# Moving weight subtractions off GpSimd and evictions ahead of weight roundings in a fused transformer layer

## The chip, the cores and the metric

The kernel runs on one core of one Trainium2 chip. A core has five engines that run side by side and meet only through semaphores: TensorE (matrix products into PSUM), VectorE (elementwise work with up to two tensors), ScalarE (activations and copies with a scale), GpSimd (elementwise work, and the queue from which adding transfers are issued) and SyncE, which issues plain transfers. The metric is the device time of one execution in microseconds. The kernel before takes 934.92 us, the median of three runs (934.16 to 937.03).

## The reference, cut to what matters

One layer of a diffusion backbone is applied to 128 context tokens and 512 latent tokens, which share all weights; the model width is 1024 and the MLP's is 4096.

```python
h = _rmsnorm(x, n1) * (1 + sc1) + sh1
aq, ak, av, bq, bk, bv, ga, gb = split(h @ w_in)          # 1024 -> 4352
a_o = _block_attention(aq, ak, av)                        # grouped-query attention
b_o = _neighbourhood_attention(bq, bk, bv, ...)           # 8 x 16 windows on the latent grid
m = sigmoid(ga) * (a_o @ w_br_a) + sigmoid(gb) * (b_o @ w_br_b)
x = x + g1 * (m @ w_out)                                  # the "out" products
h2 = _rmsnorm(x, n2) * (1 + sc2) + sh2
x = x + g2 * (square(relu(h2 @ w_mlp_in)) @ w_mlp_out)    # the MLP
y = _rmsnorm(x, final_norm_g)
```

Everything is float32. The shifts, scales and gates come from the conditioning vectors through another linear map.

## The kernel before

**Numbers in two parts.** TensorE works on a rounded form of float32. So that products keep their accuracy, each operand is held as a rounded high part and a low part, which is the rest: `hi = round(x)`, `lo = x - hi`. A product takes three matmuls: `wh*xh`, `wh*xl` and `wl*xh` (L321 to L323 and, in the MLP, L1646 to L1648). The high part is a copy on ScalarE that rounds. The low part can be made in three ways: by a subtraction on VectorE; by a subtraction on GpSimd; or by an adding transfer, for which ScalarE writes minus the rounded weight and a transfer issued by GpSimd adds the unrounded weight to it, from memory (L276) or from the staging tile (L1389).

**Tokens in two halves.** Activations lie transposed, 128 features in the partitions and 640 tokens in the free dimension, and are worked on in two halves of 320 tokens (h = 0 and 1). A matmul has 128 x 128 weights and 320 columns.

**Weights.** `W` feeds the weights of the projections, the branches and `out` in a fixed order (`w_order`). `conv` rounds one weight tile; `done` frees one and lets `ahead` round as many more as there are slots. `LOSET` (from `LOACC`) names the tiles whose low part comes by an adding transfer; `WPOOLSET` names those (`out` 4 to 7) that GpSimd subtracts.

**The out products.** The loop at L1608 takes 8 feature tiles n and both halves h: first (0,0), (0,1), (1,0) and so on to (3,1), then (4,0) to (7,0), then (4,1) to (7,1). `unit` runs the 24 matmuls of one and, in their middle and at their end, pops one entry each from the list `side`. Then `done` frees the weight (for h = 1) and thereby rounds further ones, `add_gated` (L1225) evicts the product from PSUM into the residual X1, and `sq_add` squares it on ScalarE and adds the square on VectorE to the sum `acc2` (L211), from which `rstd_half` gets the norm of that half. After (7,0) `side` holds that norm and four calls of `norm_first`, each of which scales two feature tiles of the first half (L1240), shifts them (L1246) and splits them in two parts (`cut`, L1273 and L1274). Up to here VectorE executes in the program's order (`manual_schedule`). The other engines, and VectorE from the MLP on, follow an order that a planner makes by its own estimates of when each instruction is ready.

**The MLP.** It is done in four chunks c of 1024 hidden features. In each, both layers are 2 x 2 block products that are computed with seven half-size products instead of eight (a Strassen form): A11, A12, S3, S2, A22, S1, S4, each for n = 0 to 3. A product is 12 matmuls. `FIRST0`, `FIRST1` and `FIRST2` write out their order by hand: (1,c,n,o) is one of layer 1, (2,c,n,o) one of layer 2. The right operands of S3, S2, A22 and S1 are sums of blocks; for layer 1 `t3_piece`, `t2_piece`, `t4_piece`, `t1_piece` and `n22_piece` make them from the normed halves, one feature tile k at a time, popped from `side`.

`Operands` brings the MLP's weights. Its loads come in strict order. An "A" load (SyncE, 512 KB, one of three staging tiles `wst`) holds the weights of A11 and A12. A "B" load (`wsb`, four tiles) holds a sum of weight blocks: GpSimd issues an adding transfer of 256 KB when it is loaded (L1371) and after the roundings of S3, S2 and A22 (L1394), which change it to the next product's weights. `conv` rounds one product's weights: the high part on ScalarE (L1386), the low part on VectorE or GpSimd (L1391) or by transfer (L1388, L1389). Rounding A12 or S4 frees the staging tile for the next load. Six rounded weight tiles `wb` are in flight at most. `evict` empties a product's bank, calls `ahead` for the next weights, runs what `later` has gathered and pops one entry from `side`.

Before the change GpSimd makes the low parts of A12 and A22 in layer 1 (`BLKPOOL`), 32 subtractions in all; VectorE makes the others, but for the last chunk's S4 of layer 2 (`LOTAIL`), which come by transfer.

Of the kernel before, what the change touches and what calls it, by code (L numbers as in the profile page):

```python
# [13 lines left out]
OP = mybir.AluOpType  # L14
# [5 lines left out]
KT = 8  # L20
# [32 lines left out]
NB = 4  # L53
NU = 6
NR = 5
BLKPOOL = (("A12", "A22"), ())
AUTO = (0, 0)
LAG3 = 5
POW = 0
SQP = 0  # L60
LOTAIL = tuple(("S4", n) for n in range(4))
NSUM = (1, 2)
TP = 4
TQ = 2
P3 = 8
GPV = 1
LOACC = (("in", 21, 22), ("in", 29, 30), ("in", 20, 23), ("in", 25, 26), ("in", 28, 34), ("br", 0, 8))
FINP = ()
HALVES = (slice(0, HT), slice(HT, NT))

# [2 lines left out]
def trunk_layer(ctx: ExitStack, tc: tile.TileContext, xT, small_in, wmodA, wmodB, tabs, cacheK, cacheV, bias,  # L73
                w_in, w_br, w_out, w1, w2, yT, akT, avT, bkT, bvT):
    nc = tc.nc
    PE, ACT, DVE = nc.tensor, nc.scalar, nc.vector
# [74 lines left out]
    def r32(ap):  # L151
        return ap.bitcast(F32)
# [53 lines left out]
    def sq_add(acc, x, f, sl):  # L206

        q = acc if f == 0 else u("sq")
        ACT.activation(q[:, sl], x[:, sl], AF.Square)
        if 0 < f < KT - 1:  # L210
            DVE.tensor_add(acc[:, sl], acc[:, sl], q[:, sl])  # L211
        return q

    def rstd_half(acc, last, rstd, sl):
# [19 lines left out]
    later = []  # L234
# [904 lines left out]
    class Units:  # L1139
        n = 0  # L1140
# [17 lines left out]
    for n in range(KT):  # L1158
# [4 lines left out]
        for i, w in enumerate((wa, wb)):  # L1163
            for h in range(2):
# [5 lines left out]
                ps = un.ps()  # L1170
# [51 lines left out]
    def add_gated(n, ps, h, chunk):  # L1222
        off = HALVES[h].start
        for sl, g in SEGS[h]:
            DVE.scalar_tensor_tensor(X1[n][:, sl], ps[:, sl.start - off:sl.stop - off], mod(chunk, n)[:, g:g + 1],  # L1225
                                     X1[n][:, sl], op0=OP.mult, op1=OP.add)

    T = [{}, {}, {}]
    L0, L1 = slice(0, HT), slice(HT, NT)
    RAW0, RAW1 = {}, []  # L1230

    def rstd2_half(last, h):
        return lambda: rstd_half(acc2, last, rstd2, HALVES[h])
# [37 lines left out]

    def cut(hi, lo, src):
        ACT.activation(hi, src, AF.Copy)  # L1273
        later.append(lambda: DVE.tensor_sub(lo, src, r32(hi)))  # L1274

    def cut_t(i, k, src):
        cut(T[i][k][:, L0], T[i][k][:, L1], src)
# [5 lines left out]

    def t2_piece(k):

        b11, b21, b12, b22 = RAW0[k][:, L0], RAW0[k][:, L1], RAW1[0][:, k], RAW1[0][:, k + 4]
        r = t_new(1, k)
        DVE.tensor_sub(b12, b12, b11)
        DVE.tensor_sub(r, b22, b12)
        DVE.tensor_sub(b21, b21, r)  # L1290
        cut_t(1, k, r)

    def t4_piece(k):
        cut(H2[k][0][:, L1], H2[k][1][:, L1], RAW0[k][:, L1])

    def t1_piece(k):
# [3 lines left out]
    def n22_piece(k):  # L1300
        f, b22 = k + 4, RAW1[0][:, k + 4]
        hi, lo = (t[:, L1] for t in H2[f])
        ACT.activation(hi, b22, AF.Copy, scale=-1.0)
        later.append(lambda: DVE.scalar_tensor_tensor(lo, b22, -1.0, r32(hi), op0=OP.mult, op1=OP.subtract))


    def natural(k0, sl):
# [32 lines left out]
    class Operands:  # L1340
# [38 lines left out]
        def conv(self):  # L1379
            self.feed()  # L1380
            l, c, n, o = SEQ[self.nc]
            k = (l, c, n, "A" if o in ("A11", "A12") else "B")
            t = self.st[k]
            t = t[:, 0:4] if o in ("A11", "S3", "S2", "S4") else t[:, 4:8]
            w = wp.tile([P, KT, P], F32R, tag="w" + "hl"[self.nc % 2], bufs=3, name="wb")
            ACT.activation(w[:, 0:4], t, AF.Copy)  # L1386
            if (l, c) == (2, 3) and (o, n) in LOTAIL:
                ACT.activation(w[:, 4:8], t, AF.Copy, scale=-1.0)  # L1388
                nc.gpsimd.dma_start(w[:, 4:8], t.bitcast(F32R), accum_op=OP.add)  # L1389
            else:  # L1390
                (nc.gpsimd if o in BLKPOOL[l - 1] else DVE).tensor_sub(w[:, 4:8], t, r32(w[:, 0:4]))  # L1391
            if o in ("S3", "S2", "A22"):
                e, half = {"S3": (1, 1), "S2": (0, 1), "A22": (1, 0)}[o]
                nc.gpsimd.dma_start(t, self.src(l, c, n, e)[:, 4 * half:4 * half + 4], accum_op=OP.add)  # L1394
            elif o in ("A12", "S4"):
                self.free(*k)
            self.t[SEQ[self.nc]] = w
            W.live += 1
            self.nc += 1
            self.feed()  # L1400
# [207 lines left out]
    for n, h in order(KT, 4):  # L1608
        if n not in Wt:
            Wt[n] = W.get("out", n)  # L1610
            X1[n] = o_tile(f"x1_{n}")
            nc.sync.dma_start(X1[n], xT[:, n, :])
        ps = unit(Wt[n], M, h)
        if h:
            W.done("out", n)
        add_gated(n, ps, h, 0)
        sq = sq_add(acc2, X1[n], n, HALVES[h])
        if n < KT - 4 or h == 0 and n < KT - 1:
            mod_pace(OU)
        elif n == KT - 1 and h == 0:  # L1620
            side += [rstd2_half(sq, 0)] + [lambda f=f: norm_first(f) for f in range(0, KT, 2)]
        if (n, h) == (5, 1):
            mod_step(64 - lm_n[0])
            pairs_pool()
# [187 lines left out]
```

## Time and profile before

| | us |
|---|---|
| median of three runs | 934.92 |
| the profiled execution | 934.38 |
| its span, first to last instruction | 932.6 |
| TensorE busy | 904.7 (97%) |
| VectorE busy | 718.0 (77%) |
| ScalarE busy | 572.8 (61%) |
| GpSimd busy | 218.9 (23%) |
| mean granted TensorE clock | 0.988 |

The span is what the trace shows; 1.8 us lie around it. A busy share is an average over stages: projections and attention up to about 320 us, gates and branches to 462, the out products to 508, the MLP to 922 and the last norm and stores to 932.6. TensorE is busy nearly throughout, so what matters is where it waits, and for whom. "Idle before" in a row is the engine's idle time ahead of the instruction, with what ended it.

### The profile page before, as it was taken

Reading aid. Unit: us, or ns where it says so; the run is one execution under the profiler, and the core shown is the slowest. Engines: PE = TensorE matmul, PEld = TensorE weight load, DVE = VectorE, ACT = ScalarE, POOL = GpSimd, SP = SyncE. Lnnn points to the kernel's source line nnn. Section 1 sums busy time; section 2 is a strip of 40 time slices with the busy share of each in tenths; the row PEclk is TensorE's granted clock in tenths of the full one; section 3 lists DMA queues with packets and bytes.
Section 4 is the critical chain, followed back from the end, with each engine's and each line's share of the span. In section 5 each row is a group of like instructions: output and inputs, shape, how many; then the busy total and the mean of one; then the engine's idle time right before and its main releaser. Section 6 shows DMA issues by size and latency. Waiting matters only on the chain.

```text
span 932.6 us, 16531 instructions
## 1 busy us (share of the span) xinstructions
PE 904.7 (97%) x6088; PEld 871.9 (93%) x6088; DVE 718.0 (77%) x1383; ACT 572.8 (61%) x1202; POOL 218.9 (23%) x246
## 2 busy tenths in 40 slices
PE   9999999999999999999997989999999999999996
PEld 7799889989999999999997989999999999999995
DVE  6675777857666788597786798976798868986897
ACT  4576767756667766665325768535763577447766
POOL 0020200002211011210132252344323542364130
PEclk9999999999999999999999999999999999999998
DMA  9882400126545399699746458788778887788575
GB/s 347 304 241 91 111 24 26 61 66 161 152 121 125 127 282 286 214 245 276 253 129 157 100 88 233 112 185 189 169 136 183 179 169 170 157 180 189 103 123 153
DMA packets 56449, 154.23 MB, mean 165 GB/s; under 512 B 6896, under 2 KB 10624, under 8 KB 56368
## 3 DMA queue, kind: packets, MB, share of 16 engines
q0 software_dynamic: 23776, 52.12, 32.4%
q1 hardware_dynamic: 31440, 99.74, 32.2%
q10 hardware_dynamic: 1152, 1.31, 0.4%
q8 instruction: 48, 0.79, 0.4%
q14 instruction: 33, 0.27, 0.1%
HBM read 140.82 MB, written 4.60 MB: 156 GB/s over the span
## 4 chain that ended last, share of the span: by engine, by line
PE 76%; DVE 10%; ACT 5%; issue 3%; DMA 3%; POOL 1%; DVEq 0%; SPq 0%; ACTq 0%; POOLq 0%
PE b L1646 10%; PE b L1647 10%; PE b L1648 10%; PE pg L321 6%; PE pg L322 6%; PE pg L323 6%; PE pss L322 2%; PE pss L321 2%; PE pss L323 2%; DVE wb L1391 2%; PE pt L322 2%; PE pt L321 2%; PE pt L323 2%; PE pt L700 1%; PE pss L413 1%
## 5 line engine op out<-in xcount | busy, mean ns | idle before, releaser
L1386 ACT ACTIVATE wb<-wsb 128x512 fp32r<-128x512 f32 x160 | 99.2, 628 | 99.6 <-PE b L1648 59.7
L1648 PE MATMUL b<-op,wb 128*128 128x320 f32 x448 | 138.2, 309 | 1.3 <-DVE wb L1391 1.3
L1646 PE MATMUL b<-op,wb 128*128 128x320 f32 x448 | 138.5, 309 | 0.0
L1647 PE MATMUL b<-op,wb 128*128 128x320 f32 x448 | 138.4, 309 | 0.0
L1391 DVE TENSOR_TENSOR wb<-wsb,wb 128x512 fp32r<-128x512 f32 x140 | 103.4, 742 | 35.8 <-ACT wb L1386 35.3
L1394 POOL DMA_DIRECT2D wsb<-w x96 | 84.8, 919 | 129.2 <-DVE wb L1391 94.7
L1648 PEld LDWEIGHTS b<-op,wb 128*128 128x128 f32 x448 | 84.0, 188 | 1.5 <-DVE wb L1391 1.5
L1646 PEld LDWEIGHTS b<-op,wb 128*128 128x128 f32 x448 | 84.1, 188 | 0.4 <-DVE x L1507 0.4
L1647 PEld LDWEIGHTS b<-op,wb 128*128 128x128 f32 x448 | 84.1, 188 | 0.0
L1104 DVE SCALAR_TENSOR_TENSOR mt<-wmt,cb 128x1024 f32<-128x1024 f32 x64 | 78.2, 1222 | 6.3 <-DMA wmt<-wmodB 5.1
L273 ACT ACTIVATE wh<-wst 128x512 fp32r<-128x512 f32 (+1 forms) x77 | 53.6, 711 | 28.6 <-PE pg L322 12.3
L1646 PE MATMUL b<-t,wb 128*128 128x320 f32 x192 | 59.9, 318 | 4.1 <-ACT t L1273 2.2
L1647 PE MATMUL b<-t,wb 128*128 128x320 f32 x192 | 60.8, 317 | 0.3 <-DVE t L1274 0.2
L1648 PE MATMUL b<-t,wb 128*128 128x320 f32 x192 | 60.4, 315 | 0.0
L639 DVE TENSOR_TENSOR pl<-pt,ph 128x512 fp32r<-128x512 f32 (+1 forms) x72 | 44.9, 627 | 13.6 <-ACT ph L638 13.1
L1371 POOL DMA_DIRECT2D wsb<-w x32 | 29.6, 926 | 107.4 <-DMA wsb<-w 31.2
L1386 ACT ACTIVATE wb<-wst 128x512 fp32r<-128x512 f32 x64 | 39.9, 625 | 16.1 <-PE b L1648 8.9
L638 ACT ACTIVATE ph<-pt 128x512 fp32r<-128x512 f32 (+1 forms) x72 | 39.2, 548 | 15.4 <-PE po L708 5.4
L1507 DVE SCALAR_TENSOR_TENSOR x<-b,parts,x 128x128 f32<-128x128 f32 (+1 forms) x116 | 46.1, 426 | 3.0 <-PE b L1648 2.4
L282 DVE TENSOR_TENSOR wl<-wst,wh 128x512 fp32r<-128x512 f32 (+1 forms) x50 | 35.8, 728 | 12.2 <-ACT wh L273 9.9
L1646 PEld LDWEIGHTS b<-t,wb 128*128 128x128 f32 x192 | 36.8, 194 | 5.0 <-ACT t L1273 2.5
L1507 DVE SCALAR_TENSOR_TENSOR x<-tp,parts,x 128x320 f32<-128x320 f32 (+2 forms) x60 | 39.4, 687 | 1.0 <-ACT tp L1558 1.0
(649 smaller groups left out, 2959.7 us busy)
## 6 DMA issues: line engine op xcount, KB each, us to landing
wsb<-w POOLq DMA_DIRECT2D x128, 256.0 KB, 5.2
wmt<-wmodB SPq DMA_DIRECT2D x32, 512.0 KB, 5.6
wst<-w SPq DMA_DIRECT2D x32, 512.0 KB, 4.5
wsb<-w SPq DMA_DIRECT2D x32, 512.0 KB, 4.4
wst<-w_in SPq DMA_DIRECT2D x31, 512.0 KB, 4.4
ms<-wmodA SPq DMA_DIRECT2D x16, 512.0 KB, 8.3
wl<-w_in POOLq DMA_DIRECT2D x8, 512.0 KB, 7.9
wst<-w_br SPq DMA_DIRECT2D x8, 512.0 KB, 5.0
```

The lines of the kernel that those rows point to most:

```text
L273: ACT.activation(hi[:, ks], st[:, ks], AF.Copy)
L321: PE.matmul(ps, wh[:, k], xh[:, sl], start=first, stop=False)
L322: PE.matmul(ps, wh[:, k], xl[:, sl], start=False, stop=False)
L323: PE.matmul(ps, wl[:, k], xh[:, sl], start=False, stop=last)
L1104: DVE.scalar_tensor_tensor(t, st, 1.0, cb[i], op0=OP.mult, op1=OP.mult, accum_out=mods[:, n, i:i + 1])
L1386: ACT.activation(w[:, 0:4], t, AF.Copy)
L1391: (nc.gpsimd if o in BLKPOOL[l - 1] else DVE).tensor_sub(w[:, 4:8], t, r32(w[:, 0:4]))
L1394: nc.gpsimd.dma_start(t, self.src(l, c, n, e)[:, 4 * half:4 * half + 4], accum_op=OP.add)
L1507: DVE.scalar_tensor_tensor(X1[i][:, sl], src[:, sl.start - off:sl.stop - off], g[:, j:j + 1], X1[i][:, sl], op0=OP.mult, op1=OP.add)
L1646: PE.matmul(b, w[:, k], xh, start=not whole and k == 0, stop=False, skip_group_check=True)
L1647: PE.matmul(b, w[:, k], xl, start=False, stop=False, skip_group_check=True)
L1648: PE.matmul(b, w[:, 4 + k], xh, start=False, stop=o not in ("A11", "S2", "S1") and k == 3, skip_group_check=True)
```

## The change

It has five parts. (1) In the loop of the out products `add_gated` and `sq_add` come ahead of `W.done`, and the addition of the squares is put into `later`, which is run at the start of the next unit. (2) After (7,0) an empty entry stands between any two calls of `norm_first` in `side`. (3) Once the MLP has begun, `cut` and `n22_piece` issue VectorE's half at once instead of through `later`; the subtraction that makes the raw operand of A22 (b21 minus T2) moves from `t2_piece` to `t4_piece`. (4) GpSimd subtracts no MLP weights any more. Those of layer 1's A22 go to VectorE, and those of layer 1's A12 in chunks 1 to 3 come by adding transfers from the staging tile, 12 of them; so do layer 2's A11 and A12 in chunk 0, 8, which VectorE made before, and layer 1's A12 in chunk 0, 4. The last chunk's S4 stay transfers. (5) The gate weight ("in", 31) loses its adding transfer and is subtracted on VectorE.

```diff
-BLKPOOL = (("A12", "A22"), ())
-LOTAIL = tuple(("S4", n) for n in range(4))
+LODMA = {(2, 3, "S4")} | {(1, c, "A12") for c in range(4)} | {(2, 0, "A11"), (2, 0, "A12")}
-LOACC = (("in", 21, 22), ("in", 29, 30), ("in", 20, 23), ("in", 25, 26), ("in", 28, 34), ("br", 0, 8))
+LOACC = (("in", 21, 22), ("in", 29, 30), ("in", 20, 23), ("in", 25, 26), ("in", 28, 31), ("in", 32, 34), ("br", 0, 8))
...
         if 0 < f < KT - 1:
-            DVE.tensor_add(acc[:, sl], acc[:, sl], q[:, sl])
+            later.append(lambda: DVE.tensor_add(acc[:, sl], acc[:, sl], q[:, sl]))
...
     def cut(hi, lo, src):
         ACT.activation(hi, src, AF.Copy)
-        later.append(lambda: DVE.tensor_sub(lo, src, r32(hi)))
+        rest = lambda: DVE.tensor_sub(lo, src, r32(hi))
+        rest() if RAW1 else later.append(rest)
...
     def t2_piece(k):
...
         DVE.tensor_sub(b12, b12, b11)
         DVE.tensor_sub(r, b22, b12)
-        DVE.tensor_sub(b21, b21, r)
         cut_t(1, k, r)
+        T2RAW[k] = r
 
     def t4_piece(k):
+        b21 = RAW0[k][:, L1]
+        DVE.tensor_sub(b21, b21, T2RAW[k])
         cut(H2[k][0][:, L1], H2[k][1][:, L1], RAW0[k][:, L1])
...
         ACT.activation(hi, b22, AF.Copy, scale=-1.0)
-        later.append(lambda: DVE.scalar_tensor_tensor(lo, b22, -1.0, r32(hi), op0=OP.mult, op1=OP.subtract))
+        DVE.scalar_tensor_tensor(lo, b22, -1.0, r32(hi), op0=OP.mult, op1=OP.subtract)
...
-            if (l, c) == (2, 3) and (o, n) in LOTAIL:
+            if (l, c, o) in LODMA:
                 ACT.activation(w[:, 4:8], t, AF.Copy, scale=-1.0)
                 nc.gpsimd.dma_start(w[:, 4:8], t.bitcast(F32R), accum_op=OP.add)
             else:
-                (nc.gpsimd if o in BLKPOOL[l - 1] else DVE).tensor_sub(w[:, 4:8], t, r32(w[:, 0:4]))
+                DVE.tensor_sub(w[:, 4:8], t, r32(w[:, 0:4]))
...
         ps = unit(Wt[n], M, h)
+        add_gated(n, ps, h, 0)
+        sq = sq_add(acc2, X1[n], n, HALVES[h])
         if h:
             W.done("out", n)
-        add_gated(n, ps, h, 0)
-        sq = sq_add(acc2, X1[n], n, HALVES[h])
...
-            side += [rstd2_half(sq, 0)] + [lambda f=f: norm_first(f) for f in range(0, KT, 2)]
+            side += [rstd2_half(sq, 0)]
+            for f in range(0, KT, 2):
+                side += [lambda f=f: norm_first(f), lambda: None]
+            side.pop()
```

More of the change, by code (lines that the diff above doesn't have):

```diff
@@ L1229, in trunk_layer @@
     L0, L1 = slice(0, HT), slice(HT, NT)
-    RAW0, RAW1 = {}, []
+    RAW0, RAW1, T2RAW = {}, [], {}
     def rstd2_half(last, h):
@@ L1284, in t2_piece @@
     def t2_piece(k):
-        b11, b21, b12, b22 = RAW0[k][:, L0], RAW0[k][:, L1], RAW1[0][:, k], RAW1[0][:, k + 4]
+        b11, b12, b22 = RAW0[k][:, L0], RAW1[0][:, k], RAW1[0][:, k + 4]
         r = t_new(1, k)
```

## The prediction

> **What bounds the kernel now.** I read the engine table of the page first, then TensorE's waits, then a table by stretches laid around those waits. TensorE is the bound, so only its stalls can be gained.
>
> ```profile
> PE 904.7 (97%) x6088; PEld 871.9 (93%) x6088; DVE 718.0 (77%) x1383; ACT 572.8 (61%) x1202; POOL 218.9 (23%) x246
> ```
>
> ```profile
> PE b L1646 <- DVE x L1225: 6.1, 1, 6.1
> PE b L1646 <- ACT t L1273: 2.2, 1, 2.2
> PE b L1646 <- DVE tp L1493: 1.9, 1, 1.9
> ...
> PE b L1648 <- DVE wb L1391: 1.3, 1, 1.3
> ...
> PE pg L323 <- DMA wl<-w_in: 1.0, 1, 1.0
> ```
>
> Each is a single event. In the stretches, x after PE is the number of matmuls, PEclk the granted clock, and the three columns at the end are clock, DMA share and GB/s.
>
> ```profile
> 507.50:517.50 10.00, 3.94 (x17) 3.72 (x16) 8.61 (x17) 3.90 (x10) 2.28 (x2) 0.66 0.37 107
> 543.50:552.50 9.00, 6.55 (x34) 6.02 (x33) 9.00 (x16) 3.34 (x8) 5.81 (x7) 0.81 0.89 126
> 593.50:596.00 2.50, 1.25 (x9) 0.98 (x8) 2.50 (x4) 1.40 (x2) 0.00 (x0) 1.00 0.55 93
> 636.50:645.50 9.00, 7.15 (x39) 6.89 (x38) 5.01 (x10) 5.37 (x12) 3.97 (x4) 0.81 0.91 196
> 391.00:394.00 3.00, 2.00 (x14) 1.74 (x14) 1.74 (x5) 2.97 (x5) 0.00 (x0) 1.00 0.65 122
> 643.70:914.00 270.30, 270.30 (x1842) 269.90 (x1841) 220.97 (x372) 170.12 (x310) 102.97 (x107) 1.00 0.78 161
> ```
>
> The last row is the MLP's steady state: 270.3 us for 1842 matmuls, 0.1467 us each, without a stall. Measured against that pitch (two matmuls in each count began before the stretch, so length minus (x - 2) times 0.1467), the five stretches lose 7.8, 4.3, 1.5, 3.6 and 1.2 us, together **18.4 us**. That is all that this change can win inside the matmul stream. The losses exceed the waits because TensorE comes back at half clock: PEclk is 0.66 and 0.81 where a stall of 1.9 us or more lies, 1.00 beside the 1.3 us one.
>
> [...]
>
> **The change, part by part.** *Evictions ahead.* What holds the 6.1 us wait is VectorE, whose order in the output stage is the program's:
>
> ```profile
> 500.41 2.45 DVE L1240 SCALAR_TENSOR_TENSOR raw<-x,parts,rstd 128x128 f32<-128x128 f32 x8
> ...
> 505.61 0.69 DVE L1391 TENSOR_TENSOR wb<-wst,wb 128x512 fp32r<-128x512 f32 x1 [2.15 <-ACT wb L1386]
> 506.22 0.55 DVE L1225 SCALAR_TENSOR_TENSOR x<-pg,parts,x 128x320 f32<-128x320 f32 x1
> 507.38 1.38 DVE L211 TENSOR_TENSOR acc<-acc,sq 128x320 f32<-128x320 f32 x1 [0.61 <-ACT sq L209]
> 508.68 1.23 DVE L1601 TENSOR_SCALAR parts<-parts 128x16 f32<-128x16 f32 x1
> 509.82 0.48 DVE L1274 TENSOR_TENSOR hh2l<-raw,hh2h 128x320 fp32r<-128x320 f32 x1
> ...
> 513.22 0.54 DVE L1225 SCALAR_TENSOR_TENSOR x<-pss,parts,x 128x320 f32<-128x320 f32 x1
> ```
>
> The last row is the eviction (L1225) of the last product but one, and its PSUM bank is what the first MLP product waits for. TensorE's stall begins at 507.7 and an output product is 24 matmuls, 3.5 us, so that product had been finished at 504.2, 9 us before. Ahead of its eviction stand roundings that idle 2.15 us for ScalarE, a sum of squares that idles 0.61, two instructions stretched to 1.38 and 1.23 us, and eight steps of the norm (L1240) in one go.
>
> After the change each eviction stands ahead of its unit's roundings, the sum (L211) comes a unit later, when its square is long there, and the norm groups come one a unit. I walk the new order through from 500.4: four L1240 to 501.6, eviction of (5,1) to 502.2, two roundings that still wait for ScalarE to 504.9, hh2l and hh3l (0.4 each, overlapped) and the sum to 506.1, four L1240 to 507.4, eviction of (6,1) to **507.9**, which is 0.3 us after the last output matmul instead of 6.1. The price is the norm's last group: two roundings, hh4l, hh5l and the sum, four L1240 to 511.1, eviction of (7,1), then ScalarE's shift and rounding, so that hh7l is there at 513.8. The fourth MLP product wants it at about 508 + 3 x 1.76 + 1 = 514.3. Gain **7.4** of 7.8. Bounds: 7.8, or 5.0 if these last pieces come 2.5 us later than I walk.
>
> *GpSimd's 32 subtractions go.* They run 1.3 to 1.9 us, and an instruction of VectorE that meets one is held up by it (columns: least, median and most ns):
>
> ```profile
> L1391 DVE TENSOR_TENSOR wb<-wsb,wb x140: 674/681/2240, 522.0 to 908.3; 128x512 fp32r<-128x512 f32 x140
> ...
> L1391 POOL TENSOR_TENSOR wb<-wsb,wb x16: 1284/1376/1926, 542.2 to 852.2; 128x512 fp32r<-128x512 f32 x16
> ...
> L1507 DVE SCALAR_TENSOR_TENSOR x<-tp,parts,x x60: 334/537/2445, 545.1 to 912.3; 128x320 f32<-128x320 f32 x28, 128x128 f32<-128x128 f32 x16, 128x192 f32<-128x192 f32 x16
> ```
>
> In the rows of the timelines, start and length come first, then engine and line:
>
> ```profile
> 545.07 2.44 DVE L1507 SCALAR_TENSOR_TENSOR x<-tp,parts,x 128x320 f32<-128x320 f32 x1
> 547.44 0.48 DVE L1289 TENSOR_TENSOR tp<-op 128x320 f32<-128x320 f32 x1
> 545.23 1.93 POOL L1391 TENSOR_TENSOR wb<-wsb,wb 128x512 fp32r<-128x512 f32 x1
> 547.95 0.47 ACT L1273 ACTIVATE t<-tp 128x320 fp32r<-128x320 f32 x1 [3.39 <-DVE tp L1289]
> ```
>
> That L1507 normally takes 0.54 us. So VectorE forms the T2 operand (L1289) 1.9 us late, ScalarE rounds it (L1273), and TensorE starts again at 548.4, 2.2 us after it wanted the piece. The same one stage later:
>
> ```profile
> 628.05 3.73 DVE L1507 SCALAR_TENSOR_TENSOR x<-tp,parts,x 128x128 f32<-128x128 f32 x6
> 633.83 3.44 DVE L1391 TENSOR_TENSOR wb<-wsb,wb 128x512 fp32r<-128x512 f32 x3
> 639.01 0.47 DVE L1493 TENSOR_TENSOR tp<-tp,b 128x320 f32<-128x320 f32 x1
> 633.90 1.60 POOL L1391 TENSOR_TENSOR wb<-wst,wb 128x512 fp32r<-128x512 f32 x1
> ```
>
> At the median of 0.68 (0.60 where they overlap) the three L1391 take 1.9 us, and six short L1507 about the same (0.33 each): 3.4 us of these two rows go to GpSimd, and L1493, for which TensorE waits 1.9 us, is late by that. Against it stand the 16 A22 subtractions that VectorE takes over at 0.68 us, two of them ahead of 639: 1.4 us. Net 2.0, about the whole wait; the half clock behind it goes too. Gain **2.7** of 3.6 (bounds 0 and 3.6), since the chunk's first weights also come by the new transfers.
>
> For the T2 stall VectorE gains 1.9 us, and four further subtractions (L1290) move behind T2 into t4_piece. But ScalarE, which must round the pieces, has three added activations there (0.62 us each) and the (2,0,A11) weights now come by transfers: gain **2.2** of 4.3 (bounds 0 and 4.3). That `cut` emits its VectorE half at once from here on only ranks it higher; bounds -0.5 and 0.5, I take 0, since the planner orders VectorE by readiness in this stage. The 594 stall is VectorE's backlog after layer 1; losing three subtractions (A11 3, A12 2, A12 3) just before it is 1.8 us less: gain **0.9** of 1.5 (bounds 0, 1.5). In the steady state VectorE (221 of 270 us) and ScalarE (170) have room for their additions: 0.
>
> *The gate weight ("in",31)* goes from an adding transfer to two VectorE subtractions of 0.7 us, which lie in VectorE's idle time: gain **1.0** of 1.2 (bounds 0, 1.2).
>
> *The 24 adding transfers.* Each needs a second ScalarE copy, a GpSimd issue and a landing before the low part may be used, and holds its staging tile until then. The rows: the same form at the quiet end, the same size from HBM, and the slow 512 KB one.
>
> ```profile
> DMA to landing us min/median/max: 3.2/3.3/3.3
> ```
>
> ```profile
> wsb<-w POOLq DMA_DIRECT2D x128, 256.0 KB, 5.2
> wl<-w_in POOLq DMA_DIRECT2D x8, 512.0 KB, 7.9
> ```
>
> I take 4.2 us, between 3.3 and 5.2, so a low part is there 4.7 us after the high part (0.53 for ScalarE's second copy, overlapped, + 4.2, plus GpSimd's queue) instead of 0.7 on VectorE. With six weight tiles in flight a slot that comes free is rounded (0.63) with five products of 12 matmuls, 8.8 us, still ahead: the high part leads by 8.2 us, which covers it. Two places in the first chunk have less cover:
>
> ```profile
> 537.74 0.63 ACT L1386 ACTIVATE wb<-wst 128x512 fp32r<-128x512 f32 x1
> 541.94 0.31 PE L1648 MATMUL b<-op,wb 128*128 128x320 f32 x1
> ...
> 568.40 0.69 DVE L1391 TENSOR_TENSOR wb<-wst,wb 128x512 fp32r<-128x512 f32 x1 [0.42 <-ACT wb L1386]
> 574.22 0.63 ACT L1386 ACTIVATE wb<-wst 128x512 fp32r<-128x512 f32 x1 [1.86 <-DMA wst<-w]
> 578.00 0.31 PE L1648 MATMUL b<-op,wb 128*128 128x320 f32 x1
> ```
>
> At the first (A11 of n = 2) 3.6 us lie between rounding and use; 4.7 would be 1.1 late, which falls into the T2 stall's remainder above. At the second the chain doubles. The subtraction of A12 0 frees the staging tile at 569.1, the load of A11 3 lands by 574.2, and its low part is wanted at 578.0. Afterwards: 568.4 + 0.53 + 4.2 = 573.1 free; + 5.1 load = 578.2; + 0.62 + 0.53 + 4.2 = 583.5: 5.5 us late. Behind its transfer in GpSimd's queue wait the adds (L1394) of S3, and behind its product all of TensorE, unless the planner puts A12 1 to 3 first, whose tiles are loaded. Bounds 0 and 7.2 (5.5 plus a half clock window of 1.7); I take **2.5** lost.
>
> **The sum**, against the profiled execution (934.38 us, span 932.6): 7.4 + 2.2 + 2.7 + 0.9 + 1.0 = 14.2 gained, 2.5 lost, 11.7 net: 922.7. The median of the runs shown is 0.5 above that execution: **923.2**.
>
> **Rivals.** *All five stalls close and the planner hides the transfers.* For it: VectorE alone ends four of five. 934.9 - 18.4 = 916.5.
>
> *The first stall only moves.* TensorE starts the MLP 6 us sooner, but the operands T3, T2 follow the second half's norm through VectorE and ScalarE, which are nearly full there:
>
> ```profile
> 517.30:544.00 26.70, 26.65 (x178) 26.03 (x178) 21.50 (x43) 24.23 (x57) 9.12 (x9) 1.00 0.49 91
> ```
>
> ScalarE works 24.2 of 26.7 us. If its three added copies make that chain the bound, stalls 2 and 3 stay, A11 3 loses 5.5, and 7.4 + 2.7 + 1.0 - 5.5 leaves 5.6 of the median: 929.3. Against it: the norm itself also starts 7 us sooner.
>
> *The transfers land late: slower.* GpSimd's queue is in order, and its adds (L1394) wait for VectorE:
>
> ```profile
> 627.69 0.62 ACT L1386 ACTIVATE wb<-wst 128x512 fp32r<-128x512 f32 x1
> ```
>
> The low part of that weight, A12 1 of chunk 1, is the subtraction at 633.90 above: 5.6 us after its high part. With half of that, 3 us, for A12 0 and A12 1 of chunks 1 to 3, and a landing of L, these six are L + 0.5 + 3 - 8.3 late each, and A11 3, with two landings in its chain, 2L - 2.9. At the slow row's 7.9 that is 6 x 3.1 + 12.9 = 31.5 lost against 14.2 won: 952. It decides from L = 5.7 us, where the loss is 14.2. For it: DMA share 0.78 before 24 more. Against: the median of 5.2 at that very share. [...]
>
> **How the numbers follow.** Forecast 0.47, all close 0.22, stall moves 0.20, late transfers 0.11 (half of it mild, 930 to 938). The forecast's own range is 919 to 927; for 8 in 10 I reach to both neighbours, with the runs' own 0.5 us below the lower: 916 to 931. This kernel tells 0.3%, 2.8 us, from no change. Faster: the first two and most of the third, 0.86; same 0.07; slower 0.07.
>
> **What would show it.** Right: the wait for L1225 at the first MLP product gone or under 1 us, no stretch on L1391 or L1507 beyond 1 us, PEclk 1.00 through 508 to 645. Wrong: a wait of L1648 for a DMA `wb<-wst`, or of L1646 for `wst`, in the first chunk; landings of `wb` over 6 us; TensorE still waiting for `t`.

## The result and the profile after

The changed kernel takes 959.57 us (median of four runs, 956.75 to 962.66) against 935.97 us before, a ratio of 1.0253 with a 95% interval from 1.0205 to 1.0302. The forecast, 923.2 with a range from 916 to 931, was wrong in sign. Of its rivals the late transfers came nearest (slower, 952), though not by the mechanism that it priced.

The profiled execution took 956.75 us, 22.4 more than the one of before. Two readings of the trace split this. The first matmul of the MLP starts at 504.8 us instead of 513.9, so 9.1 us were won ahead of it. From there to the MLP's last matmul 440.0 us pass instead of 408.5: its 2688 matmuls need 394.2 at 0.1467 us each, so the MLP now loses 45.8 us where it lost 14.4. TensorE's waits in the kernel after, as line, what it waited for, total us, number, longest:

```profile
PE b L1653 <- DMA wb<-wst: 9.7, 5, 3.9
PE b L1651 <- ACT op L1460: 6.9, 3, 2.7
PE b L1651 <- ACT wb L1388: 2.8, 1, 2.8
PE b L1651 <- ACT hid L1485: 2.4, 1, 2.4
PE b L1651 <- ACT hh3h L1272: 1.9, 1, 1.9
```

In these rows `op` is the rounded operand of layer 2, `hid` the hidden features, `hh3h` the high part of a piece of the normed input, and `t` and `tp` are operands formed from sums of blocks and what they are made from. L1651 to L1653 are the MLP's three matmuls, L1388 the high part, L1390 and L1391 ScalarE's second copy and the adding transfer, L1396 the adds after S3, S2 and A22 (L1394 before). The waits for the output eviction, for `t`, and for `wl<-w_in` are gone. In their place the largest is the one that the prediction had named as the sign that it was wrong: the third matmul waits for a low part that is still under way. The second is new: ScalarE is late with `op` once in each of the chunks 1 to 3. In the stretches of the kernel after, the last three columns are the clock, the DMA share and GB/s:

```profile
521.00:524.50 3.50, 3.46 (x23) 3.39 (x24) 3.50 (x9) 3.50 (x9) 0.89 (x2) 1.00 1.02 242
529.60:533.10 3.50, 3.50 (x15) 3.50 (x16) 1.31 (x4) 0.94 (x3) 0.00 (x0) 0.59 0.44 75
639.00:642.50 3.50, 3.50 (x15) 3.50 (x16) 0.00 (x0) 0.85 (x3) 0.00 (x0) 0.56 1.06 214
645.00:940.00 295.00, 285.01 (x1897) 282.20 (x1896) 220.63 (x393) 182.60 (x334) 86.02 (x99) 0.98 0.78 159
```

The last row is the stretch that ran without a stall before. Its 1897 matmuls need 278 us and take 295: 17 us are lost in the very place for which the prediction wrote 0.

What it said of VectorE holds. Its instructions in the MLP are no longer stretched (least, median and most ns; the most was 2240 for L1391 and 2445 for L1507 before):

```profile
L1393 DVE TENSOR_TENSOR wb<-wsb,wb x156: 681/691/711, 514.5 to 930.6; 128x512 fp32r<-128x512 f32 x156
...
L1509 DVE SCALAR_TENSOR_TENSOR x<-tp,parts,x x60: 341/422/559, 538.7 to 934.7; 128x320 f32<-128x320 f32 x28, 128x128 f32<-128x128 f32 x16, 128x192 f32<-128x192 f32 x16
```

And the landing of the new transfers is what it took, 4.2 us in the median (28 transfers, the last chunk's four among them; 4.5 for the 24 alone; least, median, most):

```profile
L1391 POOL DMA_DIRECT2D wb<-wst x24: 859/866/1823, 503.2 to 874.9; - x24
...
DMA to landing us min/median/max: 3.2/4.2/8.2
```

So the median was right, the gains seemed there, and yet the kernel was 24 us slower. The experiments had to tell which part cost it, and by which way.

### The profile page after: what moved, and what is told of

Its sections match the earlier page's. It is cut to its first block, busy times and chain, and to the rows that moved or that the text cites. A ratio compares the mean times of both kernels' runs of the same rounds, so it can differ in the third digit from the quotient of the medians.

```text
span 955.0 us, 16591 instructions
## 1 busy us (share of the span) xinstructions
PE 911.7 (95%) x6088; PEld 876.0 (92%) x6088; DVE 703.0 (74%) x1393; ACT 584.1 (61%) x1225; POOL 196.4 (21%) x237
## 5 line engine op out<-in xcount | busy, mean ns | idle before, releaser
L1388 ACT ACTIVATE wb<-wsb 128x512 fp32r<-128x512 f32 x160 | 99.6, 628 | 105.7 <-PE b L1653 56.6
L1651 PE MATMUL b<-op,wb 128*128 128x320 f32 x448 | 141.4, 316 | 9.7 <-ACT op L1460 6.9
L1393 DVE TENSOR_TENSOR wb<-wsb,wb 128x512 fp32r<-128x512 f32 x156 | 107.7, 691 | 57.3 <-ACT wb L1388 56.8
L1653 PE MATMUL b<-op,wb 128*128 128x320 f32 x448 | 140.2, 314 | 6.6 <-DMA wb<-wst 5.1
L1652 PE MATMUL b<-op,wb 128*128 128x320 f32 x448 | 141.1, 315 | 1.2 <-DVE op L1461 1.2
L1396 POOL DMA_DIRECT2D wsb<-w x96 | 85.6, 923 | 137.9 <-DVE wb L1393 105.4
L1651 PEld LDWEIGHTS b<-op,wb 128*128 128x128 f32 x448 | 86.3, 193 | 11.4 <-ACT op L1460 7.7
L1653 PEld LDWEIGHTS b<-op,wb 128*128 128x128 f32 x448 | 85.6, 192 | 7.6 <-DMA wb<-wst 5.9
L1652 PEld LDWEIGHTS b<-op,wb 128*128 128x128 f32 x448 | 86.2, 192 | 2.1 <-DVE op L1461 2.0
L1651 PE MATMUL b<-t,wb 128*128 128x320 f32 x192 | 60.3, 320 | 1.2 <-DVE tp L1495 1.2
L1653 PE MATMUL b<-t,wb 128*128 128x320 f32 x192 | 60.9, 317 | 0.0
L1388 ACT ACTIVATE wb<-wst 128x512 fp32r<-128x512 f32 x64 | 39.9, 625 | 29.6 <-PE b L1653 17.8
L1461 DVE TENSOR_TENSOR op<-hid,op 128x1280 fp32r<-128x1280 f32 (+2 forms) x32 | 37.0, 1155 | 3.9 <-ACT op L1460 3.6
L1651 PEld LDWEIGHTS b<-t,wb 128*128 128x128 f32 x192 | 37.4, 197 | 1.7 <-DVE tp L1495 1.5
```

The source lines that it names most:

```text
L1393: DVE.tensor_sub(w[:, 4:8], t, r32(w[:, 0:4]))
L1651: PE.matmul(b, w[:, k], xh, start=not whole and k == 0, stop=False, skip_group_check=True)
L1652: PE.matmul(b, w[:, k], xl, start=False, stop=False, skip_group_check=True)
L1653: PE.matmul(b, w[:, 4 + k], xh, start=False, stop=o not in ("A11", "S2", "S1") and k == 3, skip_group_check=True)
```

## The experiments

### Which part: the five taken apart

Four kernels take one part alone or leave one out. The first is the kernel after without its new transfers; all low parts outside the last chunk are VectorE's.

```diff
-LODMA = {(2, 3, "S4")} | {(1, c, "A12") for c in range(4)} | {(2, 0, "A11"), (2, 0, "A12")}
+LODMA = {(2, 3, "S4")}
```

> The kernel after, but its 20 low parts that newly come by adding transfers outside the last chunk are subtracted on VectorE, as all others are. Theory A (the transfers cost the time, by their own landings and by the staging tile that each holds): TensorE's waits for wb's transfers (9.7 us in the trace of after), for the rounding of A11 3 (2.8) and for late operand roundings in chunks 1 to 3 (6.9), with the half clock behind them, go: 957 minus about 27, so 928 to 932. Theory B (the earlier start of the MLP and the moved subtractions push the stalls onto ScalarE and VectorE, transfers or not): only the 9.7 us and their half clock go, 942 to 946. Theory C (VectorE, given 20 more subtractions, becomes the bound in chunk 0): over 946, with VectorE ending the waits.

Measured: 923.05 us, ratio 0.9857 (0.983 to 0.9883). Theory A holds, and by more than it expected: the time lies 5 us below its range, so more hangs on the transfers than the waits that it counted. (There are 24 of them; this expectation and a later one say 20.) TensorE's waits in this run (the MLP's first rows):

```profile
PE b L1651 <- DVE tp L1495: 3.4, 1, 3.4
PE b L1653 <- DVE wb L1393: 1.9, 2, 1.4
```

All waits for `op` and for transfers are gone, and those for `hid` and `hh3h` are 0.5 us and less: these too came with the transfers. VectorE carries 24 more subtractions without a loss in the steady state (TensorE is busy for 267.96 of the 268 us from 632 to 900); what is left lies in the change from chunk 0 to chunk 1, where the wait of 636 (`tp`) has grown to 3.4 and that of 594 (`wb`) is as before. The second puts the whole part (4) on the kernel before, with nothing else:

```diff
-BLKPOOL = (("A12", "A22"), ())
-LOTAIL = tuple(("S4", n) for n in range(4))
+LODMA = {(2, 3, "S4")} | {(1, c, "A12") for c in range(4)} | {(2, 0, "A11"), (2, 0, "A12")}
...
-            if (l, c) == (2, 3) and (o, n) in LOTAIL:
+            if (l, c, o) in LODMA:
...
-                (nc.gpsimd if o in BLKPOOL[l - 1] else DVE).tensor_sub(w[:, 4:8], t, r32(w[:, 0:4]))
+                DVE.tensor_sub(w[:, 4:8], t, r32(w[:, 0:4]))
```

> The kernel before with only the change to the weights: no subtraction of MLP weights on GpSimd, A22 on VectorE, A12 of every chunk and layer 2's A11 and A12 of chunk 0 by adding transfers. Theory A (transfers): as slow as after or slower, since the 7 us won at the start of the MLP is missing: 955 to 965. Theory B (the other parts cause much of the loss): 942 to 950.

Measured: 967.75 us, ratio 1.0336 (1.0303 to 1.0368), slower than the whole change. The parts outside (4) do not cause the loss; they hide some of it. Its list of TensorE's waits begins with the same two:

```profile
PE b L1647 <- DMA wb<-wst: 10.2, 7, 3.3
PE b L1645 <- ACT op L1457: 8.1, 4, 3.6
```

The third has parts (1) and (2) only, the fourth part (3) only, as in the diff of the change.

> The kernel before with only the output stage changed: evictions ahead of weight roundings, the sum of squares a unit later, an empty entry between two norm groups. The prediction's step: 7.4 us won, 927 to 930. Rival (the stall only moves to the operands of T3 and T2 behind ScalarE, and the GpSimd subtractions stretch VectorE as before): 932 to 936, with longer waits at about 520 to 550 us.

> The kernel before with only the order of VectorE's halves changed: they are issued at once in the MLP, and the subtraction of b21 stands in T4's step. The prediction's step: 0, between -0.5 and 0.5, so 935 to 937. Rival (b21 now stands in front of T4's operand and makes it late by the 1.9 us that TensorE waited for it in after, with the half clock 2.5): 938 to 940.

Measured: the output stage 930.96 us, ratio 0.9939 (0.9917 to 0.9962), 5.7 us won (3.6 to 7.8), between its two expectations; the order of the halves 936.35 us, 1.0006 (0.9987 to 1.0026), no difference. In the list of TensorE's waits of the output stage alone the 6.1 us wait is gone, but the next operands come late, as the rival "the first stall only moves" had it:

```profile
PE b L1649 <- ACT t L1273: 2.2, 1, 2.2
...
PE b L1649 <- ACT hh4h L1273: 1.3, 1, 1.3
...
PE b L1649 <- ACT hh6h L1273: 1.0, 1, 1.0
```

The wait for `t` stays because GpSimd is still there: at 541.92 an L1507 takes 2.44 us again. Three more kernels complete the account: GpSimd's subtractions given to VectorE, without new transfers (part (4) with `LODMA = {(2, 3, "S4")}`); the gate weight alone; and everything but the transfers and part (3).

> The kernel before, but GpSimd subtracts no weights of the MLP: VectorE subtracts A12 and A22 of layer 1 in every chunk, and no new transfer is added. The prediction's steps for the stalls of T2, 636 and 594: 2.2 + 2.7 + 0.9 = 5.8 won, 929 (928 to 931). If they add up with the other parts as measured (after without its transfers 923.1, the output stage alone 931.0 against 935.4): 923 + 4.5 + 1 to 2 for the gate weight = 929. Rival (VectorE, with 32 more subtractions, becomes the bound): 934 or more.

> The kernel before, whose gate weight (in, 31) is subtracted on VectorE. The prediction's step: 1.0 us won, so 0.9989 of before. The wait there was 1.0 us in the trace of before, 2.6 and 3.2 in those of two other kernels with the same code at that place: then 2 to 3 us, 0.997 to 0.998.

> The kernel before with the changed output stage, the gate weight (in, 31) and all MLP subtractions on VectorE, but neither the new transfers nor the changed order of VectorE's halves. That order measured 1.0006 alone, so 922 to 924, as with it; if the earlier halves were what keeps VectorE in step once GpSimd's subtractions are its own, 926 or more.

Measured: GpSimd's subtractions on VectorE 929.53 us, ratio 0.9942 (0.9921 to 0.9964), 5.4 us won (3.4 to 7.4). In its list of TensorE's waits the one for T2's `t` is gone and that of 636 is down from 1.9 to 0.7; that of 594 is still 1.4, and the wait for the eviction (L1224) stays, as it should. No L1506 there takes longer than 0.55 us, where the same line of before (L1507) took up to 2.45. Its row of 545.07, 2.44 us long, shows no wait ahead: the hold-up by GpSimd's subtraction lies in the instruction itself and not at a semaphore. The rows of TensorE's waits:

```profile
PE b L1645 <- DVE x L1224: 4.7, 1, 4.7
...
PE b L1647 <- DVE wb L1390: 1.4, 1, 1.4
...
PE b L1645 <- DVE tp L1492: 0.7, 1, 0.7
```

The gate weight: 0.9997 (0.9982 to 1.0012); its wait is gone from the trace; 1.0 us can neither be confirmed nor excluded, but the 2 to 3 us of the second expectation are. Together without part (3): 923.40 us, ratio 0.988 (0.9848 to 0.9912), the same as with it. These two, at 923, beat both kernels.

### Which transfers

The costs below are the ratio less 0.9857, times 935 us; they are uncertain by some 3 us. First, after with only layer 2's eight in chunk 0, then with only the twelve of layer 1's A12 in chunks 1 to 3.

```diff
-LODMA = {(2, 3, "S4")} | {(1, c, "A12") for c in range(4)} | {(2, 0, "A11"), (2, 0, "A12")}
+LODMA = {(2, 3, "S4"), (2, 0, "A11"), (2, 0, "A12")}
```

```diff
-LODMA = {(2, 3, "S4")} | {(1, c, "A12") for c in range(4)} | {(2, 0, "A11"), (2, 0, "A12")}
+LODMA = {(2, 3, "S4")} | {(1, c, "A12") for c in range(1, 4)}
```

> The kernel after, of whose new transfers only the 8 of layer 2's A11 and A12 in chunk 0 are left; the 12 of layer 1's A12 are subtracted on VectorE. The trace of after shows 8.8 us lost at these products (2.0, 0.9, 2.6 and 3.2), and some 2 us of half clock behind. If the losses lie where the trace shows them, 923 + 11 = 934 (931 to 937). If one transfer's cost falls mostly on later loads (the strict order), less: 925 to 930.

> The kernel after, of whose new transfers only the 12 of layer 1's A12 in chunks 1 to 3 are left. The prediction's rival had 3.1 us for each of six of them, 923 + 18.6 = 942. The prediction's sum had their cost at 0 (a lead of 8.2 us covers them): 923 to 925. The trace of after: waits at 634.7, 679.9, 784.7 and 885.9 lose 4.1, 3.7, 2.4 and 3.7 us, and the half clock some 3: 923 + 17 = 940 (936 to 944).

Measured: 935.28 us, ratio 0.9984 (0.9963 to 1.0005), and 942.98 us, 1.0083 (1.0051 to 1.0115). So eight transfers cost 12 us and twelve cost 21; the prediction had 2.5 and 0. Of the whole loss of 37 us some 4 are left for the four of chunk 0's layer 1, which were not tried alone. Then the twelve by their n, with an `if` on n beside the test on `LODMA`: n = 0 alone, n = 3 alone, n = 1 and 2.

```diff
-            if (l, c, o) in LODMA:
+            if (l, c, o) in LODMA or l == 1 and c and o == "A12" and n == 3:
```

> The kernel after without its new transfers, but for the three of layer 1's A12, n = 0, in chunks 1 to 3, whose products waited 3.5, 0.0 and 0.8 us for the landing in the run with all 12. Theory L: these are the costly ones, 923 + 4.3 + 2 to 4 of half clock and followers = 929 to 931, and the waits for op go with the nine others only if those were late themselves. Theory H: each of the 12 costs about the same through the next loads, 923 + 20 x 3/12 = 928, and waits for op are seen although n = 2 and 3 are subtracted.

> The kernel after without its new transfers, but for the three of layer 1's A12, n = 3, in chunks 1 to 3. Theory Q (A12 3's transfer takes the place of S3's add in GpSimd's queue, and with it the operand is late): the three waits for op return, 1.4 to 2.3 us each, with 0.7 behind each and some half clock: 923 + 8 to 12 = 931 to 935, and the add of S3 (L1396) lands 9 us after ScalarE's rounding, as there. Rival (lateness adds up over all transfers of a chunk): 923 + 20 x 3/12 = 928, waits for op under 1 us.

> The kernel after without its new transfers, but for the six of layer 1's A12, n = 1 and 2, in chunks 1 to 3. Theory Q: these displace nothing that is awaited, 923 to 926. Rival (lateness adds up): 923 + 20 x 6/12 = 933.

Measured: n = 0: 928.23 us, 0.9917 (0.9899 to 0.9935), 6 us for three transfers; n = 1 and 2: 925.38, 0.9868 (0.9833 to 0.9902), 1 us for six; n = 3: 939.32, 1.0003 (0.9977 to 1.0029), 14 us for three for which no product waits, 4 us above its expectation's range (its ten executions spread from 934 to 942, and the profiled one took 940.6). Together that is 20, which agrees with the 21 of all twelve. So there are two mechanisms, one at n = 0 and a larger one at n = 3.

### By which way: the awaited landing, the held tile, the queue

Two theories were tried on the kernel after. L: each low part itself comes too late. H: the staging tile, held until the landing, delays the next loads. The first kernel lets the 24 transfers add from memory, so that ScalarE's copies free the tile; the second adds into a spare tile that nobody reads, and VectorE makes the low part.

```diff
+                raw = t
+                if c != 3 or l == 1:
+                    raw = self.src(l, c, n, 0)[:, 0:4] if o == "A11" else self.src(l, c, n, 0)[:, 4:8]
-                nc.gpsimd.dma_start(w[:, 4:8], t.bitcast(F32R), accum_op=OP.add)
+                nc.gpsimd.dma_start(w[:, 4:8], raw.bitcast(F32R), accum_op=OP.add)
```

```diff
+                ACT.activation(w[:, 4:8], t, AF.Copy, scale=-1.0)
+                nc.gpsimd.dma_start(spare, t.bitcast(F32R).rearrange("p a b -> p (a b)")[:, 0:504], accum_op=OP.add)
+                DVE.tensor_sub(w[:, 4:8], t, r32(w[:, 0:4]))
```

> The kernel after, but the 20 new transfers add the raw weight from device memory and not from the staging tile, which is then free once ScalarE has read it twice; the landing is still awaited. Theory H (the staging tile that a transfer holds delays the next loads in the strict order, and the late loads stop ScalarE and so the operands): most of the loss goes, 926 to 934. Theory L (each low part itself comes too late for its product): 950 to 962, since the landing is no shorter from memory (5.7 us against 4.5).

> The kernel after, but the 20 new transfers add the staging tile (252 of its 256 KB) to a spare tile that nobody reads; the low part is subtracted on VectorE. ScalarE's second copy, GpSimd's issue, the traffic and the held staging tile stay, only the product no longer waits for the landing. Theory H (held tile): 940 to 957. Theory L (late low part): 923 to 930.

Measured: from memory 961.11 us, ratio 1.0264 (1.0233 to 1.0294), as after. Freeing the tile wins nothing in total, but the trace moves between the two kinds of wait: from memory the landing is longer, 6.4 us in the median and 10.9 at most (4.2 and 8.2 in after), and in TensorE's waits those for the landing grow to 24.6, while those for `op` fall to 2.9:

```profile
PE b L1656 <- DMA wb<-w: 24.6, 8, 5.8
PE b L1654 <- ACT op L1463: 2.9, 3, 1.0
```

The unread transfers gave 940.01 us (1.0052, 1.003 to 1.0073), the lower edge of theory H's range, and this run is no clean test: there is one spare tile, so 14 of the 24 transfers waited for the one before, 41.3 us in all, and the adds queued behind them. In chunks 1 to 3 that matters less (6 waits, 17.2 us), so the run was made again with those twelve alone.

> The kernel after without its other new transfers, whose 12 transfers of layer 1's A12 in chunks 1 to 3 add into a spare tile that nobody reads; the low part is subtracted on VectorE, so ScalarE's second copy, GpSimd's issue, the traffic and the held staging tile stay and only the product's wait goes. With the wait it was 943.0, without the transfers 923.1. Theory L (the awaited landing is what costs): 923 to 927. Theory H (held tile and a fuller GpSimd queue make the next weights and with them the operands late): 932 to 943.

Measured: 925.14 us, ratio 0.9894 (0.9866 to 0.9923). That looks like theory L, but the spare tile's rows (its transfers, then what ended GpSimd's idle time before them) show that the edit did not do what its expectation said:

```profile
L1395 POOL DMA_DIRECT2D spare<-wst x12: 864/864/1222, 570.2 to 823.6; - x12
...
  DMA wst<-w: 18.0, 5
```

Depending on no copy, the transfers could go when the load (`wst<-w`) landed, ahead of ScalarE's rounding, and so hardly held the tile longer. The run shows little more than the traffic, 3.5 us by its ratio, which the noise does not tell from nothing. The next one was meant to put them behind ScalarE's copy again, since they add into a tile that the copy has just written:

```diff
+            if l == 1 and c and o == "A12":
+                spare = u("spare", F32R)[:, 0:512].rearrange("p (k n) -> p k n", k=4)
+                ACT.activation(spare, t, AF.Copy, scale=-1.0)
+                nc.gpsimd.dma_start(spare, t.bitcast(F32R), accum_op=OP.add)
+                DVE.tensor_sub(w[:, 4:8], t, r32(w[:, 0:4]))
```

> As the run with the 12 unread transfers of chunks 1 to 3 (925.1 us), but each adds into a tile that ScalarE's second copy has just written, so it cannot be issued ahead of that copy: ScalarE's copy, GpSimd's place in the queue, the traffic and the held staging tile are those of the run with the 12 awaited transfers (943.0 us), only the product does not wait, since VectorE makes its low part. Theory L (the product's own wait, and all that follows from it): 923 to 927. Theory H (held tile and queue make the next weights and with them ScalarE's operand roundings late): the waits for op in chunks 1 to 3 return, 6.0 us and some 4 of half clock: 931 to 940.

Measured: 923.58 us, ratio 0.9867 (0.9851 to 0.9884), though the transfers take long to land:

```profile
L1392 POOL DMA_DIRECT2D spare<-wst x12: 864/1208/1940, 570.4 to 842.6; - x12
...
DMA to landing us min/median/max: 4.6/5.8/8.5
```

This looks like the end of theory H, but it is no clean test either. The second copy now writes the spare tile and so needs only the load, and the planner draws it and its transfer ahead of the rounding of the weight. In chunk 1 the transfer of n = 0 goes at 570.45 and its weight is rounded at 614.71, that of n = 2 at 627.81 against 634.15, and that of n = 3 at 643.70 against 649.19. Only the staging tile of n = 1 is held long after its rounding, from 618.42 until the landing at 628.1, and the next load goes at 628.26.

The better test is the run with n = 1 and 2 above. Its transfers are issued behind the rounding and hold their tiles: in chunk 1 the weights are rounded at 617.73 and 633.87, the transfers land at 626.8 and 640.6, and the next loads go at 626.92 and 640.71. These six cost 1 us in all, so for n = 1 and 2 theory H falls. For n = 0 and n = 3 no run separates the held tile from the wait and from the place in GpSimd's queue. The place does differ in the run with unread transfers: there that of n = 3 is out 8.5 us ahead of the add that follows the rounding of S2 3 (652.22), while with all twelve awaited it goes at 656.70, ahead of that add at 658.83.

### Two ways to be late

For n = 0 the trace shows the wait itself. The timeline of after, start and length first, about the A12 0 of chunk 1 (GpSimd, then ScalarE, then TensorE):

```profile
628.11 0.86 POOL L1396 DMA_DIRECT2D wsb<-w  x1 [3.39 <-DVE wb L1393]
628.64 1.22 POOL L1373 DMA_DIRECT2D wsb<-w  x1
629.59 2.05 POOL L1396 DMA_DIRECT2D wsb<-w  x2
630.74 1.82 POOL L1391 DMA_DIRECT2D wb<-wst  x1
...
628.37 0.62 ACT L1388 ACTIVATE wb<-wst 128x512 fp32r<-128x512 f32 x1
628.89 0.62 ACT L1390 ACTIVATE wb<-wst 128x512 fp32r<-128x512 f32 x1
...
638.96 0.42 PE L1653 MATMUL b<-hh4h,wb 128*128 128x320 f32 x1 [3.94 <-DMA wb<-wst]
```

The second copy is done at 629.5, the transfer stands fifth in GpSimd's queue and goes at 630.74, and it lands at 638.91, 8.2 us later. The trace's times for this and five others, in us:

```
after            high part  2nd copy ends  issued   landed   3rd matmul   high part to landing
(1,1,0) A12       628.37       629.51      630.74   638.91     638.96         10.5
(1,2,0) A12       736.98       738.13      740.33   746.67     746.72          9.7
(1,3,0) A12       838.97       840.12      841.82   847.89     847.93          8.9
(2,0,0) A12       562.47       564.32      568.04   573.55     573.60         11.1
(1,1,3) A12       668.21       669.71      670.00   673.34     675.52          5.1
(1,3,3) A12       873.08       874.58      874.87   878.88     881.47          5.8
```

(The times of the high part are its starts; it takes 0.6 us.) In chunk 1 the third matmul was due at 634.86, when the one ahead of it had run, 5.9 us after the end of the high part; in chunks 2 and 3 the same lead is 8.3. In the run with n = 0 alone these waits come to 2.8 of the 6 us.

For n = 3 it is the queue. These transfers land in time, 5.1 and 5.8 us after the high part. But in the run with n = 3 alone the timeline shows this of GpSimd, and below of ScalarE, in chunk 1:

```profile
654.84 0.87 POOL L1391 DMA_DIRECT2D wb<-wst  x1 [4.74 <-ACT hid L1477]
656.44 0.86 POOL L1373 DMA_DIRECT2D wsb<-w  x1 [0.73 <-DVE tp L1498]
656.97 1.22 POOL L1396 DMA_DIRECT2D wsb<-w  x1
...
664.05 0.63 ACT L1388 ACTIVATE wb<-wsb 128x512 fp32r<-128x512 f32 x1 [4.14 <-DMA wsb<-w]
664.59 0.46 ACT L1476 ACTIVATE hid<-tp 128x320 f32<-128x320 f32 x1
...
666.78 0.47 ACT L1460 ACTIVATE op<-hid 128x320 fp32r<-128x320 f32 x1
```

The L1396 at 656.97 is the add that follows the rounding of S2 3 and makes the weights of S4 3 (the expectation of this run calls it S3's, by mistake). It is third in the queue and lands at 663.97, 7.0 us after its issue; without new transfers (the two rows below) it goes out ahead of the next load's add and lands after 4.5.

```profile
652.98 0.86 POOL L1396 DMA_DIRECT2D wsb<-w  x1 [5.34 <-DVE wb L1393]
653.64 1.09 POOL L1373 DMA_DIRECT2D wsb<-w  x1
```

Its issue is 4.0 us later too, of which 2.8 are the whole stretch (A12 3 is rounded at 652.79 instead of 649.96). ScalarE, whose order is fixed, waits 4.14 us for it, and behind that wait stand the relu of hidden features (L1476) and the rounding of the operand (L1460), for which TensorE waits. Chunks 2 and 3 look alike: ScalarE idles 4.32 and 3.75 us there. If this is so, S4 3 one product later takes the wait off ScalarE without touching a transfer:

```diff
-    FIRST2 = [("A11", 0), ("S1", 3, 1), ("A11", 1), ("S4", 3, 1), ("A12", 0), ("A12", 1),
+    FIRST2 = [("A11", 0), ("S1", 3, 1), ("A11", 1), ("A12", 0), ("S4", 3, 1), ("A12", 1),
```

> As the run with only the three transfers of A12, n = 3 (939.3 us), but S4 (n = 3) of layer 1 stands one product later in the order of chunks 1 to 3, behind layer 2's A12 0. Theory Q (S2's add lands late behind A12 3's transfer, and ScalarE waits for it ahead of the relu of A12 3): ScalarE has 1.8 us more until it wants that weight, and the waits for op fall below 1 us or go: 924 to 931. Rival (the transfers delay the operand in another way, by the second copy or the held tile): 935 to 941.

> The control: the same order without any new transfer outside the last chunk (923.1 us with the old order). Both theories: 921 to 925, as no wait for op is left there to win.

Measured: 928.18 us, ratio 0.9904 (0.9888 to 0.9921), against 939.32 with the old order; the control 923.64, 0.9864 (0.9847 to 0.9881), unchanged. Nine of the 14 us come back by this alone. The waits for `op` fall from 5.1 to 2.5 us. ScalarE's waits for that add are now 1.49, 3.12 and 0.41 us in chunks 1 to 3, and TensorE's for `op` follow them: 0.43, 2.05 and none. So the cure is complete only in chunk 3. Of the 4 to 5 us that remain, the wait of 2.05 is the same mechanism; the rest is open, the held tile included. The row of TensorE's waits with n = 3 alone, and then with the new order:

```profile
PE b L1651 <- ACT op L1460: 5.1, 3, 2.0
```

```profile
PE b L1651 <- ACT op L1460: 2.5, 2, 2.1
```

## Why the prediction was wrong, point by point

**What bounds the kernel, and the stalls.** TensorE was the bound (busy for 97% of the span before, 95% after), and the matmul stream held the gain. Three of the five stalls close (the eviction, T2, the gate weight). That of 594 stays at 1.4 us in the kernel after and without its transfers, and that of 636, which the prediction put down to GpSimd, is 0.6 to 3.4 us where neither GpSimd's subtractions nor new transfers are left, with VectorE behind it each time.

**The gains.** They added up to 14.2. The kernel after without its new transfers won 13.4 us (10.9 to 15.9, from its ratio), so the sum was right, partly by luck, since two terms were shared out wrongly. *Evictions ahead*: 7.4 predicted, 5.7 alone (3.6 to 7.8), since TensorE then meets ScalarE's late roundings, as the rival said (1.3 us for `hh4h`, 1.0 for `hh6h`); these go once GpSimd's subtractions go too (0.2 and 0.3 in the kernel after without its new transfers). *GpSimd's subtractions*: 2.2 + 2.7 + 0.9 predicted, 5.4 (3.4 to 7.4) measured, though the 0.9 did not come. *`cut` at once*: 0, measured 0. *The gate weight*: 1.0, too small to be told.

**The 24 adding transfers: the step that failed.** 2.5 us were taken, 37 were lost. Two sentences carried that term.

The first was that the low part is there 4.7 us after the high part, against a lead of 8.2. The landing of 4.2 was right in the median, and the lead was 8.3 at A12 0 of chunks 2 and 3, but only 5.9 in chunk 1, where the longest wait lies. And the products meet single transfers, not the median, and where GpSimd's adds bunch, as at A12 0, each piece was longer: the second copy ends 1.1 us after the high part begins, the queue takes 1.2 to 2.2, and the landing 6.1 to 8.2. That makes 8.9 to 10.5 from the start of the high part, 8.3 to 9.9 from its end, where 4.7 stood. This is what the third rival had described, and its limit on the landing, 5.7 us, was tested against the wrong number: it should have been held against the landings at those places. It costs 6 us in chunks 1 to 3, and with layer 2's eight in chunk 0, the chain of A11 3 among them, 12 more. The 1.7 us of half clock in the prediction's upper bound for A11 3 are an estimate: at the waits of 6.1 and 1.9 us of before, 7.8 and 3.6 were lost, 1.7 more each. No run shows them for A11 3 by itself. In the kernel after, the 3.5 us from 578.7, behind its wait of 2.84, have a granted clock of 0.50.

The second was that in the steady state the lead "covers it", so 0. This counted only the products whose weights the transfers make. The larger loss, 14 us, comes from three transfers that were in time: they stand ahead of another add in GpSimd's queue, and the late weight blocks ScalarE (4.14, 4.32 and 3.75 us in chunks 1 to 3), whose operand was due next. Nine of these 14 us are shown to go that way, by the changed order. The prediction named what is queued behind a transfer for A11 3 of chunk 0 alone, and did not ask it for the others.

A third belief fell unasked: it wrote that a transfer "holds its staging tile until then", as a cost. The chain of A11 3 did cost TensorE 2.8 us at 576. The six transfers of n = 1 and 2 held theirs and cost 1 us together, which the noise doesn't tell from nothing; for n = 0 and 3 a price is not shown.

**The rivals.** "The first stall only moves" was half right for the output stage alone. "Late transfers" had the sign, 952, with the queue and the waiting products, but not the blocked ScalarE. **The signs named in advance** worked: L1653 waiting for `wb<-wst` is the first row of the waits. The chance of slower, 0.07, was far too low for a change that adds 24 asynchronous steps to GpSimd's queue, whose price the trace of before shows: GpSimd idles 3.51 us for the add at 633.28, while the subtraction behind it (633.90) has had its high part since 628.3.

## What to carry to other kernels

Cost an asynchronous step by its worst place and not by its median: the landing where the queue is fullest, set against the lead of that very product. Then ask of each issue what stands behind it in its queue, and who waits for that; here three transfers that were themselves in time cost 14 us, and the three late ones of the same product 6. And take a change of several parts apart early: without the new transfers this one was worth 13 us, and the transfers took 37.

## What the runs showed of the hardware

**Seven adds issued in a bunch landed one after the other.** In the run with unread transfers, seven adds issued 0.54 us apart from 600.48 us on landed at 606.53, 607.81, 609.28, 610.55, 611.84, 613.15 and 614.42, about 1.3 us apart (1.27 to 1.47); the last, 256 KB like the others, took 10.7 us:

```profile
DMA to landing us min/median/max: 3.8/5.6/10.7
```

What spaced them is not shown. By the author's estimate it may be no more than the traffic: 256 KB every 1.3 us is 200 GB/s, nearly all that the core moved from 606.5 to 614.4 (204 GB/s at a DMA share of 1.06).

**The granted clock did not go by the length of a wait alone.** The prediction had half clock after waits of 1.9 us or more. In the kernel before, behind the wait of 6.05 us, the starts of the matmuls from 514.57 to 516.71 lie 0.27 us apart, where the steady state has 0.1467. In the kernel after:

```profile
529.59 0.41 PE L1653 MATMUL b<-op,wb 128*128 128x320 f32 x1 [1.88 <-DMA wb<-wst]
...
521.04 0.42 PE L1651 MATMUL b<-hh4h,wb 128*128 128x320 f32 x1 [2.40 <-ACT hid L1485]
```

The wait of 1.88 us is followed by a stretch at 0.59 of the clock, the longer one of 2.40 by one at 1.00 (the stretches from 529.60 and 521.00 above); after 3.94 us it is 0.56. So a shorter wait cost clock here and a longer one did not; what decides it no run shows.
